# ScalarE decays retention's keys, the pairs' late products move to other PSUM banks, the solve follows retention's masks, and the chain loads a chunk ahead

## The chip, the cores and the metric

The kernel runs on one core of a Trainium2 chip. The metric is the device time of one execution in microseconds (us), the median of several runs.

## What is computed

One layer of a decoder: the input x (2048 tokens of 1024 numbers) is normalised, projected by one large matrix, and split among five branches (retention, GLA, a state-space branch, RWKV-7, attention into a memory); each branch's output is gated, projected up, weighted by a sigmoid gate, summed, projected out and added to x, and a last norm follows. The change touches retention and RWKV-7:

```
# retention, by chunks of 128 (one decay per head and step)
scores = einsum('bhntd,bhnsd->bhnts', qc, kc) * seg          # seg: the causal decay mask
y_intra = einsum('bhnts,bhnsv->bhntv', scores, vc)
chunk_state = einsum('bhnsd,bhnsv->bhndv', kc * exp(last - cum)[..., None], vc)   # decayed keys
y_inter = einsum('bhntd,bhndv->bhntv', qc * exp(cum)[..., None], prev)
# RWKV-7, one step per token
sa = einsum('bhvk,bhk->bhv', state, a_t)
state = state * w_t + sa[..., None] * b_t + v_t[..., None] * k_t
y_t = einsum('bhvk,bhk->bhv', state, r_t)
```

The kernel computes RWKV-7 by chunks of 64 tokens, so that the steps inside a chunk become a triangular system per head and chunk.

## The kernel before, in words

The 2048 tokens are worked in four groups of 512. Inside a group the order of the program is: memory attention; the preparation of RWKV-7's four pairs of heads (`rwkv_prep`); retention (`ret`, rotary of q, rotary of k, the value projection `v_tok`, then two pairs of heads, 0 and 1); the pairs' systems (`rwkv_sys`); RWKV-7's chain over eight chunks (`rwkv_chain`); the state-space branch; GLA; the output. Matmuls are full float32, made of three reduced ones over a high and a low part, so that a projection of one tile of 128 columns is 24 matmuls of 128x512 and a projection up from a branch is 6 on a half. Between the steps `fill(n)` takes n pieces of waiting work (gate projections with their tanh on ScalarE, and up projections, whose product VectorE merges into the tiles mg) off two lists, so that TensorE has something to do while other engines work.

- **Preparation.** For each pair, `rwkv_prep` projects k and r, then multiplies w2a2 into two PSUM banks of the pool br (L1108 to L1112), from which ScalarE and VectorE make the decays, the scaled a, b, k, r (tiles kb and ar, stored to DRAM as kbd and ard for the chain), and projects v. What is left for a pair, `late()` (L1158), runs inside the next pair's turn: 16 small matmuls into a bank (ap), which VectorE masks into ab (L299); a sum over heads into another bank (bps), which VectorE multiplies by v (L299); and four transposes of v into a third.
- **The solve.** When the last late is done, `rwkv_solve` sets up the triangular systems of 32x32 blocks, and 31 steps (n = 1 to 31) run on VectorE, each a product over n x n elements (L299 through `tt`) and a sum over it (L1206), both on tiles blk. `solve(n)` puts n steps into the program at the places where `ret` calls it: 4 (the setting up counts as one), 4, 6, then in each pair 4 and 6, and what is left at the start of `rwkv_sys`.
- **Retention's pairs.** For each pair `ret` makes qh on VectorE, transposes k into a br bank, multiplies by the decay kd into kt (L768, two VectorE instructions of 128x256 out of PSUM), makes the chunk states sp (TensorE, from kt), scores (TensorE), four states S and two masked scores (VectorE), y (TensorE), and in `finish_pair` two gate projections and, for each head, a sum of squares and a chain of ten VectorE instructions of 128x512 (L339, L329, L299, L302), whose result ScalarE casts (L378) and GpSimd splits.
- **The pairs' systems.** `rwkv_sys` transposes the solve's result twice (VectorE, L1222 and L1224), copies the parts (ScalarE and GpSimd, L1229), calls fill for 2 and 3 pieces, and joins the halves with 32x32 matmuls: lower, a VectorE copy zs (L1240), corner.
- **The chain.** In each chunk c, `rwkv_chain` issues loads of kbd, ard and vtd on the queue of the sync engine (SP), right before it uses them (L1271 to L1275).

What stands on each engine is not written by hand: a scheduler takes the program's instructions with their dependences and lays out one order per engine, and every engine works through its own in that order. PSUM has eight banks: a pool acc of three, br of three and y of two; a tile of a pool waits until the readers of the bank that it takes are done. SBUF's tiles s come from a pool of 42.

Names in the rows: L305 is the one line that issues all matmuls, L317 all transposes, L299 and L302 the VectorE products, L296 ScalarE's functions, L378 and L379 the split into high and low part (ScalarE, then GpSimd), L689 and L693 the GpSimd parts of the rotary, wt the weights' tiles (kw: their copy in DRAM, made in group 0 and loaded in groups 1 to 3).

## Time and profile before

| | |
|---|---|
| median of 3 runs | 3621.07 us (3617.41 to 3624.74) |
| the profiled execution's own time | 3618.59 us |
| its span | 3616.7 us |
| TensorE busy | 3428.6 us (95%) |
| VectorE, ScalarE, GpSimd busy | 55%, 28%, 25% |
| mean granted TensorE clock | 0.967 of full speed |

The profiled execution is 2.5 us below the median. To read the profile: idle time of TensorE is the span less its busy time, 188 us; a wait line tells which instruction of which engine ended such an idle stretch. PEclk is the TensorE clock that was granted, as a share of full speed; where it is below 1, busy time is longer than the same work takes at full speed.

### The profile page before, as it was taken

Reading aid. Unit: us, or ns where it says so; the run is one execution under the profiler, and the core shown is the slowest. Engines: PE = TensorE matmul, PEld = TensorE weight load, DVE = VectorE, ACT = ScalarE, POOL = GpSimd, SP = SyncE. Lnnn points to the kernel's source line nnn. Section 1 sums busy time; section 2 is a strip of 40 time slices with the busy share of each in tenths; the row PEclk is TensorE's granted clock in tenths of the full one; section 3 lists DMA queues with packets and bytes.
Section 4 is the critical chain, followed back from the end, with each engine's and each line's share of the span. In section 5 each row is a group of like instructions: output and inputs, shape, how many; then the busy total and the mean of one; then the engine's idle time right before and its main releaser. Section 6 shows DMA issues by size and latency. Waiting matters only on the chain.

```text
span 3616.7 us, 52010 instructions
## 1 busy us (share of the span) xinstructions
PE 3428.6 (95%) x20368; PEld 2760.3 (76%) x20368; DVE 1993.1 (55%) x3180; ACT 997.8 (28%) x1821; POOL 914.8 (25%) x919
## 2 busy tenths in 40 slices
PE   7879998998999899999999899999999989999998
PEld 6767777777777777888877787788887777778887
DVE  6785456635467645653357844554346674555243
ACT  5433224342343111312133121222123311131212
POOL 3665235555333110201103210021101411020110
PEclk9989899999999999999999999999999999999999
DMA  6665556576766454555565554445465654454555
GB/s 211 212 221 203 202 174 227 197 258 219 271 218 216 137 177 140 171 172 169 186 202 195 181 162 149 162 150 185 157 222 188 204 162 158 140 165 147 173 169 192
DMA packets 269541, 673.17 MB, mean 186 GB/s; under 512 B 27232, under 2 KB 81008, under 8 KB 269296
## 3 DMA queue, kind: packets, MB, share of 16 engines
q1 hardware_dynamic: 268864, 669.32, 55.6%
q8 instruction: 161, 2.64, 0.3%
q14 instruction: 84, 0.69, 0.1%
q10 hardware_dynamic: 432, 0.52, 0.1%
HBM read 503.54 MB, written 162.00 MB: 184 GB/s over the span
## 4 chain that ended last, share of the span: by engine, by line
PE 55%; DVE 10%; issue 1%; DMA 1%; ACT 1%; POOL 0%; SPq 0%; DVEq 0%; POOLq 0%; ACTq 0%
PE acc L305 44%; PE br L305 6%; PE y L305 4%; DVE s L302 4%; DVE s L299 2%; DVE blk L299 2%; DVE blk L1206 1%; PE br L317 1%; DMA s<-ard 1%; ACT s L296 1%; DVE s L339 0%; DVE s L329 0%; DMA s<-in_xT_dram 0%; ACT blk L1171 0%; DMA s<-kmd 0%
## 5 line engine op out<-in xcount | busy, mean ns | idle before, releaser
L305 PE MATMUL acc<-xhi,wt 128*128 128x512 f32 x5632 | 1820.9, 399 | 15.4 <-ACT s L296 9.6
L305 PEld LDWEIGHTS acc<-xhi,wt 128*128 128x128 f32 x5632 | 1071.5, 191 | 256.6 <-ACT s L296 12.3
L305 PE MATMUL acc<-xlo,wt 128*128 128x512 f32 x2816 | 1120.5, 398 | 2.5 <-DVE xlo L1552 1.8
L305 PEld LDWEIGHTS acc<-xlo,wt 128*128 128x128 f32 x2816 | 538.8, 191 | 117.2 <-DVE xlo L1552 3.0
L305 PE MATMUL acc<-s,wt 128*128 128x512 f32 (+1 forms) x2448 | 597.8, 394 | 15.1 <-DVE s L302 7.3
L305 PEld LDWEIGHTS acc<-s,wt 128*128 128x128 f32 x2448 | 456.3, 190 | 113.6 <-ACT wt L378 13.9
L302 DVE SCALAR_TENSOR_TENSOR s<-s,acc 128x512 f32<-128x512 f32 x192 | 131.6, 685 | 666.4 <-PE acc L305 360.7
L379 POOL TENSOR_TENSOR wt<-wr,wt 128x512 fp32r<-128x512 f32 (+1 forms) x256 | 354.8, 1391 | 380.1 <-ACT wt L378 369.3
L302 DVE SCALAR_TENSOR_TENSOR s<-s,s 128x512 f32<-128x512 f32 (+1 forms) x458 | 366.9, 805 | 31.9 <-ACT s L296 19.8
L379 POOL TENSOR_TENSOR s<-s,s 128x512 fp32r<-128x512 f32 x120 | 159.7, 1339 | 816.6 <-ACT s L378 672.3
L296 ACT ACTIVATE s<-acc 128x512 f32<-128x512 f32 x232 | 136.3, 595 | 593.4 <-PE acc L305 593.3
L305 PE MATMUL br<-s,s 64*64 64x64 f32 (+6 forms) x2432 | 213.1, 281 | 47.9 <-DVE s L768 26.9
L305 PEld LDWEIGHTS br<-s,s 64*64 64x64 f32 (+3 forms) x2432 | 164.3, 168 | 97.6 <-issue 39.8
L378 ACT CAST wt<-wr 128x512 fp32r<-128x512 f32 (+1 forms) x256 | 155.2, 611 | 268.3 <-PE acc L305 89.6
L1416 POOL TENSOR_TENSOR mg<-mg,s 128x512 f32<-128x512 f32 x64 | 87.2, 1362 | 548.6 <-DVE s L302 548.6
L378 ACT CAST s<-s 128x512 fp32r<-128x512 f32 x182 | 112.8, 620 | 341.4 <-DVE s L302 316.6
L296 ACT ACTIVATE s<-s 128x512 f32<-128x512 f32 (+1 forms) x204 | 119.3, 611 | 293.3 <-DVE s L299 114.1
L299 DVE TENSOR_TENSOR s<-s,s 128x512 f32<-128x512 f32 (+2 forms) x186 | 144.2, 803 | 44.5 <-ACT s L296 42.2
L299 DVE TENSOR_TENSOR s<-s 128x512 f32<-128x512 f32 (+1 forms) x167 | 163.0, 980 | 5.8
L305 PE MATMUL y<-s,s 128*64 128x64 f32 (+4 forms) x2112 | 137.2, 254 | 7.5 <-DVE s L299 4.9
L305 PE MATMUL acc<-wt,xhi 128*128 128x512 f32 x384 | 124.3, 404 | 19.0 <-DMA wt<-kw 9.0
L305 PEld LDWEIGHTS y<-s,s 128*64 128x64 f32 (+2 forms) x2112 | 113.4, 152 | 37.5 <-DVE s L1311 11.4
(220 smaller groups left out, 3202.5 us busy)
## 6 DMA issues: line engine op xcount, KB each, us to landing
wt<-kw SPq DMA_DIRECT2D x712, 512.0 KB, 3.3
kw<-wt SPq DMA_DIRECT2D x240, 512.0 KB, 3.0
wr<-in_wg_dram SPq DMA_DIRECT2D x176, 256.0 KB, 3.8
s<-in_xT_dram SPq DMA_DIRECT2D x88, 256.0 KB, 5.0
ard<-s SPq DMA_DIRECT2D x32, 256.0 KB, 2.2
kbd<-s SPq DMA_DIRECT2D x32, 256.0 KB, 2.7
s<-kbd SPq DMA_DIRECT2D x32, 256.0 KB, 4.1
s<-ard SPq DMA_DIRECT2D x32, 256.0 KB, 4.7
```

Of the source, the lines that this page charges most:

```text
L296: self.nc.scalar.activation(out, in_, f, bias=bias, scale=scale, **kw)
L299: self.nc.vector.tensor_tensor(out, a, b, op)
L302: self.nc.vector.scalar_tensor_tensor(out, a, s, b, op0, op1)
L305: i = self.nc.tensor.matmul(out, lhsT=lhsT, rhs=rhs, start=start, stop=stop)
L317: self.nc.tensor.transpose(out, in_, self.c["ident"])
L378: self.nc.scalar.copy(hi, src)
L379: (eng or self.nc.gpsimd).tensor_tensor(lo, src, hi.bitcast(F32), ALU.subtract)
L1206: nc.vector.tensor_reduce(X[:, s_, s_ + 1:], pv, AX.X, ALU.add)
L1416: (eng or self.pick({"ret": 0, "rwkv": 1, "ssd": 2, "gla": 3}[key])).tensor_tensor(merged[d], merged[d], t, ALU.add)
```

## The change

Four edits. The key decay of retention (L768) becomes two ScalarE activations with a scale instead of two VectorE multiplies. In `rwkv_prep` the w2a2 matmuls come before late, late's two banks that VectorE reads are taken from the pool y instead of br, and the first late has 2 pieces of fill ahead of it instead of 1. The first step of the `solve(4)` of a pair (step 14 in pair 0, step 24 in pair 1) carries a dependence on the pair's last mask, for the scheduler's order alone. The chain's three loads are issued one chunk ahead.

```diff
--- before.py
+++ after.py
@@ -280,7 +280,7 @@
 
     NS = 42
 
-    FILL = {"mem": (2, 0, 2, 2, 1, 1, 3, 3), "ret": (1, 3, 0), "late": (1, 1, 1, 1), "sys": (2, 3), "chain":
+    FILL = {"mem": (2, 0, 2, 2, 1, 1, 3, 3), "ret": (1, 3, 0), "late": (2, 1, 1, 1), "sys": (2, 3), "chain":
             (2, 3, 2, 1, 1, 2, 4, 3), "norm": 0, "ssd": (6, 0, 3, 4, 4), "gla": (3, 1, 2, 3, 1), "eng": (0, 1,
             0, 1, 0, 1, 0, 0, 1, 1, 1, 1, 1), "rope": (3, 3), "solve": (4, 4, 6, 4, 6)}
 
@@ -296,7 +296,7 @@
         self.nc.scalar.activation(out, in_, f, bias=bias, scale=scale, **kw)
 
     def tt(self, out, a, b, op):
-        self.nc.vector.tensor_tensor(out, a, b, op)
+        return self.nc.vector.tensor_tensor(out, a, b, op)
 
     def stt(self, out, a, s, b, op0, op1):
         self.nc.vector.scalar_tensor_tensor(out, a, s, b, op0, op1)
@@ -765,7 +765,7 @@
             for j in range(2):
                 h = 2 * p + j
                 v4 = lambda t: t.rearrange("p (c h d) -> p c h d", h=2, d=64)[:, :, j, :]
-                nc.vector.tensor_scalar(v4(kt), v4(tp), self.c["kd"][:, h:h + 1], None, ALU.mult)
+                self.act(v4(kt), v4(tp), AF.Copy, scale=self.c["kd"][:, h:h + 1])
 
             sp = self.ps("br")
             for c in range(4):
@@ -780,11 +780,11 @@
             for j, sps in enumerate(self.scores(k[p], q[p])):
                 pt = self.s()
                 h = 2 * p + j
-                self.tt(pt.rearrange("p (c t) -> p c t", t=P), sps.rearrange("p (c t) -> p c t", t=P),
+                i = self.tt(pt.rearrange("p (c t) -> p c t", t=P), sps.rearrange("p (c t) -> p c t", t=P),
                         self.c["dec"][:, h * P:(h + 1) * P].unsqueeze(1).to_broadcast([P, 4, P]), ALU.mult)
                 pts.append(pt)
             ys = [self.ps("y") for _ in range(2)]
-            self.solve(K.FILL["solve"][3])
+            self.solve(K.FILL["solve"][3], i)
             self.fill(K.FILL["ret"][0])
             for j in range(2):
                 for c in range(4):
@@ -1102,14 +1102,14 @@
             k = self.shift(4 + p)
             sq = self.squares(k, self.p["k_k"][:, pc], self.pick(6))
             r = self.shift(p)
-            if late:
-                self.fill(K.FILL["late"][i - 1])
-                late()
             wps, aps = self.ps("br"), self.ps("br")
             for t0 in range(0, T, 256):
                 t_ = slice(t0, t0 + 256)
                 self.mm(wps[:, t_], self.w2a2[0:64, cs_], wa[0:64, t_])
                 self.mm(aps[:, t_], self.w2a2[64:128, cs_], wa[64:128, t_])
+            if late:
+                self.fill(K.FILL["late"][i - 1])
+                late()
             pw = self.s()
             self.act(pw, wps, AF.Tanh, bias=self.hw0[:, pc], scale=0.5)
             nc.vector.tensor_scalar(pw, pw, 1.0, None, ALU.add)
@@ -1157,7 +1157,7 @@
 
             def late(i=i, p=p, rk=rk, v=v, ars=ars, kbs=kbs):
 
-                ap = self.ps("br")
+                ap = self.ps("y")
                 for c in range(8):
                     for q in range(2):
                         rq = slice(64 * q, 64 * q + 64)
@@ -1170,7 +1170,7 @@
                     rg, b = slice(32 * g, 32 * g + 32), g % 2
                     (nc.scalar.copy, nc.gpsimd.tensor_copy)[g % 2](
                         dia[rg, :, i * 8:i * 8 + 8], ab[rg, :, 32 * b:32 * b + 32].rearrange("s j t -> s t j"))
-                bps = self.ps("br")
+                bps = self.ps("y")
                 self.msum(bps, self.bones_r, rk)
                 bv = self.s()
                 self.tt(bv, bps, v, ALU.mult)
@@ -1198,19 +1198,22 @@
         nc.vector.memset(Xf[:, ::33], 1.0)
         prf = pr.rearrange("p s t -> p (s t)")
 
-        def step(s_):
+        def step(s_, after=None):
             n = 31 - s_
             pv = prf[:, 0:n * n].rearrange("p (c t) -> p c t", t=n)
-            self.tt(pv, X[:, s_ + 1:, s_ + 1:].rearrange("p t c -> p c t"),
+            i = self.tt(pv, X[:, s_ + 1:, s_ + 1:].rearrange("p t c -> p c t"),
                     blk[:, s_ + 1:, s_].unsqueeze(1).to_broadcast([P, n, n]), ALU.mult)
             nc.vector.tensor_reduce(X[:, s_, s_ + 1:], pv, AX.X, ALU.add)
-
-        return X, [lambda s_=s_: step(s_) for s_ in range(30, -1, -1)]
-
-    def solve(self, n=99):
+            if after is not None:
+                self.order(i, after)
+
+        return X, [lambda after=None, s_=s_: step(s_, after) for s_ in range(30, -1, -1)]
+
+    def solve(self, n=99, after=None):
         for _ in range(n):
             if self.dq:
-                self.dq.pop(0)()
+                self.dq.pop(0)(after)
+                after = None
 
     def rwkv_sys(self, Ab, X):
 
@@ -1266,13 +1269,20 @@
             b = self.s()
             nc.sync.dma_start(b, self.bvd[p])
             BV.append(b)
-        for c in range(8):
-            S = self.S_rw
+        def operands(c):
             AR, KB = self.s((P, 4, P)), self.s((P, 4, P))
             nc.sync.dma_start(KB, self.kbd[c])
             nc.sync.dma_start(AR, self.ard[c])
             UV = self.s((P, 8, 64))
             nc.sync.dma_start(UV[0:64], self.vtd[c * 64:c * 64 + 64, :, :].rearrange("t p (q d) -> t (p q) d", q=2))
+            return AR, KB, UV
+
+        nxt = operands(0)
+        for c in range(8):
+            S = self.S_rw
+            AR, KB, UV = nxt
+            if c < 7:
+                nxt = operands(c + 1)
             As = []
             aps = [self.ps("br") for _ in range(2)]
             for p, q, h, r in heads:
@@ -1364,7 +1374,7 @@
         Ab, dia, gC, late = self.rwkv_prep(wa, range(4))
         X = []
 
-        def begin():
+        def begin(_):
             late()
             x, self.dq = self.rwkv_solve(dia)
             X.append(x)
```

**TensorE, preparation of group 1, around the last pairs' w2a2.** Before, four products of late (64x64 and the sums over bones_r) stand ahead of w2a2 and all use br:

```order
L305 MATMUL br_2135_9860<-s_2110_9717,s_2111_9718 64x64 x8
L305 MATMUL br_2135_9860<-s_2112_9726,s_2113_9727 64x64 x8
L305 MATMUL br_2137_9883<-s_2103_9696,bones_r_441 128x512
L305 MATMUL br_2137_9883<-s_2104_9697,bones_r_441 128x512
L317 MATMUL br_2139_9889<-cst_76,s_2118_9768 128x128 x4
L305 MATMUL br_2141_9897<-s_1978_9088,w2a2_115 128x256 x2
L305 MATMUL br_2142_9898<-s_1978_9088,w2a2_115 128x256 x2
L305 MATMUL br_2152_9927<-s_2125_9809,bones_r_441 128x512
L305 MATMUL br_2152_9927<-s_2126_9810,bones_r_441 128x512
```

After, here one pair earlier, w2a2 comes first, a piece of fill (s is a branch's output, wt a weight) behind it, and then late in banks y:

```order
L305 MATMUL br_2088_9633<-s_1978_9088,w2a2_115 128x256
L305 MATMUL br_2089_9634<-s_1978_9088,w2a2_115 128x256
L305 MATMUL acc_2091_9641<-s_1940_8901,wt_2090_9639 128x512
L305 MATMUL acc_2091_9641<-s_1941_8902,wt_2090_9639 128x512
L305 MATMUL acc_2091_9641<-s_1940_8901,wt_2090_9639 128x512
L305 MATMUL acc_2091_9641<-s_1972_9049,wt_2090_9639 128x512
L305 MATMUL acc_2091_9641<-s_1973_9050,wt_2090_9639 128x512
L305 MATMUL acc_2091_9641<-s_1972_9049,wt_2090_9639 128x512
L305 MATMUL y_2093_9650<-s_2066_9501,s_2067_9502 64x64 x8
L305 MATMUL y_2093_9650<-s_2068_9510,s_2069_9511 64x64 x8
L305 MATMUL y_2095_9673<-s_2059_9480,bones_r_441 128x512
L305 MATMUL y_2095_9673<-s_2060_9481,bones_r_441 128x512
```

What moved: w2a2 no longer stands behind matmuls whose banks VectorE reads, and the fill stands between the two.

**VectorE, group 1, where retention's pair 0 begins.** Before, the solve's steps run to n = 30 ahead of qh (s<-s,cst) and the key decay (L768), and step 31 (128x961) right behind:

```order
L299 TENSOR_TENSOR blk_2194_10153<-blk_2193_10152,blk_2192_10150 128x900
L1206 TENSOR_REDUCE blk_2193_10152<-blk_2194_10153 128x30
L299 TENSOR_TENSOR s_2227_10390<-s_2166_9998,cst_76 128x512
L768 TENSOR_SCALAR s_2229_10397<-br_2228_10392,cst_76 128x4x64 x2
L302 SCALAR_TENSOR_TENSOR mg_2241_10448<-s_2087_9631,acc_2240_10441 128x512
L299 TENSOR_TENSOR blk_2194_10153<-blk_2193_10152,blk_2192_10150 128x961
L302 SCALAR_TENSOR_TENSOR s_2231_10409<-Sret_523_2368,cst_76,br_2230_10400 128x128
L1206 TENSOR_REDUCE blk_2193_10152<-blk_2194_10153 128x31
```

After, the steps stop after n = 13 (128x169): the four products of rotary k, qh, the four states (Sret) and the two masks follow, and step 14 (128x196) only behind these:

```order
L299 TENSOR_TENSOR blk_2197_10164<-blk_2196_10163,blk_2195_10161 128x169
L1206 TENSOR_REDUCE blk_2196_10163<-blk_2197_10164 128x13
L299 TENSOR_TENSOR s_2208_10237<-s_2200_10175,s_1922_8815 128x512
L299 TENSOR_TENSOR s_2209_10238<-s_2201_10176,s_1919_8804 128x512
L299 TENSOR_TENSOR s_2211_10247<-s_2201_10176,s_1922_8815 128x512
L299 TENSOR_TENSOR s_2212_10248<-s_2200_10175,s_1919_8804 128x512
L299 TENSOR_TENSOR s_2230_10401<-s_2170_10029,cst_76 128x512
L302 SCALAR_TENSOR_TENSOR s_2234_10420<-Sret_528_2384,cst_76,br_2233_10411 128x128
L302 SCALAR_TENSOR_TENSOR s_2234_10420<-s_2234_10420,cst_76,br_2233_10411 128x128 x2
L302 SCALAR_TENSOR_TENSOR Sret_2235_10421<-s_2234_10420,cst_76,br_2233_10411 128x128
L299 TENSOR_TENSOR s_2238_10436<-br_2236_10426,cst_76 128x512
L299 TENSOR_TENSOR s_2239_10438<-br_2237_10427,cst_76 128x512
```

What moved: steps 14 to 31 from ahead of pair 0 to behind it. Of these, steps 14 to 23 stand between pair 0's masks and its finish, and steps 24 to 31 behind pair 1's masks.

**VectorE, group 1, at the end of the solve.** After, the last step, the two transposes (L1225 and L1227 in the new numbering) and the start of pair 1's finish are interleaved; mg_2352 is the merge that frees the bank of acc_2351:

```order
L299 TENSOR_TENSOR blk_2197_10164<-blk_2196_10163,blk_2195_10161 128x961
L302 SCALAR_TENSOR_TENSOR s_2329_10909<-s_2328_10907,acc_2327_10882 128x512
L339 TENSOR_SCALAR s_2332_10915<-br_2330_10911 128x512
L1206 TENSOR_REDUCE blk_2196_10163<-blk_2197_10164 128x31
L329 TENSOR_SCALAR s_2331_10914<-s_2332_10915 128x512
L1225 STREAM_TRANSPOSE blk_2353_11005<-blk_2196_10163 128x1024
L299 TENSOR_TENSOR s_2333_10917<-s_2331_10914 128x512
L1227 STREAM_TRANSPOSE blk_2354_11007<-blk_2196_10163 128x1024
L302 SCALAR_TENSOR_TENSOR s_2333_10917<-s_2333_10917,s_2332_10915 128x512
L302 SCALAR_TENSOR_TENSOR s_2331_10914<-s_2333_10917,s_2331_10914 128x512
L302 SCALAR_TENSOR_TENSOR mg_2352_11003<-s_2310_10812,acc_2351_10996 128x512
L299 TENSOR_TENSOR s_2333_10917<-s_2331_10914 128x512
```

Before, the solve and its transposes were done ahead of pair 0's finish, and none of this stood beside pair 1's.

**ScalarE, group 1.** After, the new key decay of pair 1 (from br_2289, with the scale from cst) stands behind the two casts that end pair 0's finish:

```order
L378 CAST s_2278_10646<-s_2277_10644 128x512
L378 CAST s_2286_10668<-s_2285_10666 128x512
L296 ACTIVATE s_2290_10691<-br_2289_10686,cst_76 128x4x64 x2
```

and at the end of retention the copies of the solve's parts (L1232, L1229 before) and the two casts that end pair 1's finish stand ahead of the tanh of acc_2348:

```order
L296 ACTIVATE s_2328_10907<-acc_2327_10882 128x512
L1232 COPY s_2047_9440<-blk_2353_11005 32x8x32 x2
L1232 COPY s_2094_9667<-blk_2353_11005 32x8x32 x2
L1232 COPY s_2142_9914<-blk_2353_11005 32x8x32 x2
L1232 COPY s_2190_10141<-blk_2353_11005 32x8x32 x2
L378 CAST s_2336_10929<-s_2335_10927 128x512
L378 CAST s_2344_10951<-s_2343_10949 128x512
L296 ACTIVATE s_2349_10992<-acc_2348_10967 128x512
L296 ACTIVATE s_2361_11065<-acc_2360_11040 128x512
L296 ACTIVATE s_2365_11096<-acc_2364_11071 128x512
```

What moved: the decay from VectorE into ScalarE's order, and the eight copies from before retention's finish to here. TensorE's order behind retention's y of pair 1 is: projections acc_2322 and acc_2327 (24 each), four sums of squares, acc_2348 (24), acc_2351 and acc_2356 (6 each), acc_2360 and acc_2364 (24 each), then the systems' lower; acc_2360 waits for a VectorE reader of a bank and acc_2364 for a ScalarE reader.

## Rows read from the trace of the kernel before

**Rows 1.** The page, its first part: busy microseconds of an engine, its share of the span, its instructions.

```profile
PE 3428.6 (95%) x20368; PEld 2760.3 (76%) x20368; DVE 1993.1 (55%) x3180; ACT 997.8 (28%) x1821; POOL 914.8 (25%) x919
```

**Rows 2.** The waits of TensorE over the whole span: who was waited for, us in total, how often, the longest.

```profile
PE br L305 <- DVE s L768: 26.9, 5, 6.2
PE br L305 <- DVE s L299: 25.0, 12, 5.5
PE acc L305 <- DMA wt<-kw: 9.2, 6, 2.4
PE br L305 <- DMA s<-ard: 7.4, 10, 1.5
PE br L305 <- POOL s L1149: 6.3, 2, 3.1
```

**Rows 3.** Windows over the four preparations of the pairs (group 0 to 3): start and end, length, busy us and count of each engine, PEclk (the mean granted clock), share of the DMA engines, GB/s.

```profile
98.00:214.00 116.00, 105.01 (x545) 83.50 (x545) 90.45 (x112) 54.66 (x94) 85.10 (x95) 0.93 0.69 230
1052.00:1159.00 107.00, 102.82 (x541) 82.30 (x541) 80.92 (x119) 37.08 (x64) 46.45 (x67) 0.98 0.68 220
1909.00:2023.00 114.00, 106.39 (x561) 85.08 (x561) 83.55 (x123) 38.88 (x65) 46.72 (x68) 0.96 0.65 212
2779.00:2893.00 114.00, 106.25 (x553) 84.93 (x553) 83.58 (x123) 38.85 (x65) 46.73 (x68) 0.96 0.64 212
```

**Rows 4.** The waits of TensorE in three of these windows, the first, second and third group's, one line of each (the fourth has the same line as the third).

```profile
PE br L305 <- DVE s L299: 9.4, 3, 5.5
PE br L305 <- DVE s L299: 3.8, 2, 2.9
PE br L305 <- DVE s L299: 2.9, 1, 2.9
```

**Rows 5.** Windows in group 1, columns as in rows 3: around retention's first pair; as the pairs' systems begin.

```profile
1202.00:1213.00 11.00, 6.74 (x36) 5.40 (x37) 10.24 (x16) 0.00 (x0) 0.00 (x0) 0.53 0.04 17
1291.00:1298.00 7.00, 7.00 (x93) 5.44 (x88) 2.73 (x7) 1.85 (x6) 0.00 (x0) 0.52 0.55 189
```

**Rows 6.** The waits in the stretch of retention's value projection: two lines of TensorE's in group 0 (230 to 266 us), and one of GpSimd's in group 1 (1171 to 1198 us).

```profile
PE acc L305 <- POOL wt L379: 5.4, 3, 4.2
PE acc L305 <- ACT wt L378: 2.2, 1, 2.2
POOL s L689 <- DVE s L299: 13.3, 1, 13.3
```

**Rows 7.** The timeline of VectorE in group 1: start, us, engine, line, operation, out<-in. The solve's steps are the pairs of L299 and L1206 on blk; 128x196 is step 14, 128x576 step 24, 128x961 step 31.

```profile
1170.76 0.53 DVE L299 TENSOR_TENSOR blk<-blk,blk 128x196 f32<-128x196 f32 x1
1188.03 1.13 DVE L299 TENSOR_TENSOR blk<-blk,blk 128x576 f32<-128x576 f32 x1
1205.73 0.87 DVE L768 TENSOR_SCALAR s<-br,cst 128x256 f32<-128x256 f32 x2
1209.87 1.15 DVE L1206 TENSOR_REDUCE blk<-blk 128x31 f32<-128x961 f32 x1
1212.92 2.02 DVE L1222 STREAM_TRANSPOSE blk<-blk 128x1024 f32<-128x1024 f32 x1
1214.86 1.20 DVE L1224 STREAM_TRANSPOSE blk<-blk 128x1024 f32<-128x1024 f32 x1
```

**Rows 8.** The timeline of VectorE where retention is finished: the first row, a middle one and the last of the second head's chain of pair 1, in group 1 and then in group 0.

```profile
1280.29 0.68 DVE L339 TENSOR_SCALAR s<-br 128x512 f32<-128x512 f32 x1
1282.54 1.42 DVE L302 SCALAR_TENSOR_TENSOR s<-s,s 128x512 f32<-128x512 f32 x2
1286.95 0.69 DVE L302 SCALAR_TENSOR_TENSOR s<-s,s 128x512 f32<-128x512 f32 x1
356.05 0.68 DVE L339 TENSOR_SCALAR s<-br 128x512 f32<-128x512 f32 x1
359.57 3.36 DVE L302 SCALAR_TENSOR_TENSOR s<-s,s 128x512 f32<-128x512 f32 x2
366.97 0.69 DVE L302 SCALAR_TENSOR_TENSOR s<-s,s 128x512 f32<-128x512 f32 x1
```

**Rows 9.** ScalarE in group 1: a cast and a tanh from a PSUM bank (timeline), and a group of instructions of the whole span that reads 128x256 from PSUM (busy us, mean ns of one).

```profile
1255.27 0.62 ACT L378 CAST s<-s 128x512 fp32r<-128x512 f32 x1 [7.56 <-DVE s L302]
1270.62 0.60 ACT L296 ACTIVATE s<-acc 128x512 f32<-128x512 f32 x1 [3.41 <-PE acc L305]
L1294 ACT COPY rs<-br 128x256 f32<-128x256 f32 x32 | 11.9, 372 | 48.0 <-PE br L305 48.0
```

**Rows 10.** The timeline of TensorE in group 1, retention's pair 1: two matmuls of a projection with two others between them; states and scores; the first half of y.

```profile
1251.86 0.39 PE L305 MATMUL acc<-xlo,wt 128*128 128x512 f32 x1
1252.54 0.39 PE L305 MATMUL acc<-xlo,wt 128*128 128x512 f32 x1
1256.94 2.95 PE L305 MATMUL br<-s,s 128*64 128x128 f32 x32
1261.08 2.05 PE L305 MATMUL y<-s,s 128*128 128x128 f32 x16
```

**Rows 11.** Windows, columns as in rows 3: retention of group 0 and of group 1, and the start of the pairs' systems of group 0.

```profile
266.00:366.00 100.00, 88.03 (x516) 71.33 (x514) 60.49 (x72) 32.15 (x58) 54.18 (x45) 0.91 0.60 204
1198.00:1286.00 88.00, 81.76 (x424) 66.84 (x422) 52.75 (x76) 16.77 (x28) 14.12 (x15) 0.94 0.45 141
366.00:382.00 16.00, 13.31 (x183) 10.53 (x184) 7.34 (x16) 5.12 (x12) 2.56 (x2) 0.57 0.61 192
```

## The prediction

> **What bounds the kernel now.** I read the page first: TensorE is busy 95% of the span, 3428.6 of 3616.7 us [rows 1], so time can be won only from its 188 us of idle time and from the stretches in which a stall is followed by a lowered clock. Then its waits: the largest are for the key decay (26.9 us in 5 waits), for VectorE's masks while TensorE wants a br bank (25.0 in 12), for weights from DRAM (9.2), the chain's loads (7.4) and GpSimd's part of late's operands (6.3) [rows 2]. The change aims at each of them. Then windows, for the clock: around the wait for the key decay in group 1 the mean granted clock is 0.53, and TensorE is busy 6.74 us of 11 [rows 5]; at about half speed (1.2 instead of 2.4 GHz), 0.47 x 6.74 = 3.2 us of that busy time would not be there at full speed. So a stall of 6 us costs about 9. I price each clock loss so: (1 - PEclk) x busy.
>
> **A. Preparation.** w2a2 waits for a br bank because late's two products hold two of three until VectorE has read them, and VectorE is behind. The four windows hold 11.0, 4.2, 7.6 and 7.8 us of idle time (length less PE busy), 30.5 in all, and 7.4 + 2.1 + 4.3 + 4.3 = 18.1 us of clock loss [rows 3]. After, w2a2 stands ahead of late, and late uses y. The upper bound is thus 48.6 us; the lower is the named waits alone, 9.4 + 3.8 + 2.9 + 2.9 [rows 4] + 6.3 (POOL s L1149, covered by the added piece of fill) [rows 2] = 25.3. The named stalls sit inside most of the lowered stretches, so I take 38. A piece of fill taken here is missing later, but it is work that has to be done anyway; cost nil.
>
> **B. Value projection.** In group 1, GpSimd's rotary part waits 13.3 us for VectorE [rows 6], whose four products stand among solve steps; the rotary's stores stand in SP's queue ahead of the weights, so TensorE then waits for wt. After, step 13 is the last ahead of these products, and steps 14 to 23, from 1170.76 to 1188.03 [rows 7], are out of their way. TensorE's waits: most of the 9.2 us for wt<-kw [rows 2] and 5.4 + 2.2 in group 0 [rows 6], 16.8; with a clock loss in group 0 that I don't see apart it could be 22, and if the loads themselves are late, 0. I take 17. The chain's prefetch adds no load here: its loads come later in SP's order.
>
> **C. Retention's pairs.** For pair 0 the decay ran at 1205.73, behind step 30 [rows 7]. After, it is on ScalarE, ahead of the whole queue of steps. A read of 128x256 from PSUM takes ScalarE 372 ns [rows 9], VectorE 0.43 (0.87 for two [rows 7]): the engine itself changes nothing, only the queue does. Of the 26.9 us [rows 2], four waits (22.7) are pair 0's; four clock losses of 3.2 go with them: -35.5, and about 0.8 per group comes back for transposes, decay and states in a row, +3: -32.
>
> For pair 1, the decay on ScalarE stands behind two casts that need the end of pair 0's finish. That finish, on VectorE, is two chains of some 7.4 us (1280.29 to 1287.64 for such a one [rows 8]) with a merge between, 15.7, then cast 0.62 [rows 9] and two decays, 0.74: 17.1 us after the sums of squares. TensorE's work from there to the states is now two projections and two 6-matmul pieces, 60 matmuls at 0.68/3 = 0.227 us each [rows 10], 13.6. So TensorE waits about 2.6 (17.1 less 13.6 and less 0.9 for transposes and the late start), then about 1.2 for the masks (states and scores take 2.95, y starts 4.1 after them with four matmuls between [rows 10]), and loses about 1.7 of clock: +5.5 in groups 1 to 3. In group 0 a wait and clock loss of 7.5 is there already; I get 12: +4.5. Together +21.
>
> **D. The pairs' systems, the new cost.** Let t1 be the end of pair 1's masks. VectorE then has steps 24 to 31 (1188.03 to 1211.02 less 2.7 for what stood between [rows 7]: 20.3), two merges and two finish starts (2.4), the transposes with two rows between (2.02 + 1.20 + 1.1 [rows 7]), two products (1.4), then mg_2352 (0.6): t1 + 29. TensorE does y (2.05 for one half [rows 10], 1.0 for the smaller one, an estimate), two projections of 24 matmuls (5.45 each at 0.227), four sums of squares, one projection and two pieces: 3.1 + 10.9 + 0.9 + 5.45 + 2.7 = 23.0, and acc_2360 then waits for mg_2352: 6.4 to 7. VectorE's rest of two chains ends 11 us later, t1 + 40; cast 0.62 and tanh 0.60 [rows 9], so acc_2364's bank is free at t1 + 41.3, while acc_2360 was done at t1 + 34.9: 6.4 more. Clock loss behind the second stall 3.2; zs and corner 0.6. Against it stands the lowered clock of before, 0.48 x 7.0 = 3.4 [rows 5]. Net 7 + 6.4 + 3.2 + 0.6 - 3.4 = +13.8 in groups 1 to 3. In group 0 the chains are slower, 11.6 us against 7.35 for the second [rows 8]; with 7 us more for both and the steps, and 8.4 of stall and clock there before (2.7 idle and 0.43 x 13.31 [rows 11]), I take +14.5. Together +56.
>
> Here lies the rule that speaks against the change. The row order shows the decay and the tanh behind casts that wait for VectorE, though their own operands are ready; the trace shows such a cast only after an idle stretch of 7.56 us that VectorE ended [rows 9].
>
> The Trainium skill, PSUM — Partial Sum Buffer, Engine vs sequencer instructions, says that ScalarE's and VectorE's queues are strictly first in, first out. By that rule the tanh waits out both chains, as in my sum. Were a ready instruction let past, the sum would lose 6.4 + 3.2 in four groups, some 38 us.
>
> **E. Chain.** Loads a chunk ahead remove most of 7.4 us [rows 2]; bounds 0 and 10 with clock; I take 6. The loads move ahead of 2 or 3 weight loads of fill in SP's queue; 512 KB land in about 3 us each by the page, and the pieces have a projection's time in hand: nil.
>
> **Sum.** -38 - 17 - 32 + 21 + 56 - 6 = -16 against the profiled 3618.6: 3602.6; the median is 2.5 above that execution, so **3605**. A measurement tells 0.2%, 7.2 us, from no change.
>
> **Rivals.**
>
> *Slower: retention's chains run at group 0's pace in every group.* In group 0 two products of two SBUF tiles take 3.36 us where GpSimd splits weights beside them, in group 1 1.42 [rows 8]. After, the eight GpSimd copies of the solve's parts fall beside pair 1's chains, and each chain now sits on TensorE's path. If all of group 0's slowdown came, 4.3 us for the second chain [rows 8], 2 for the first, 2 for the steps and 4 where the decay waits, it were +12.3 in three groups: 3605 + 37 = **3642**. It decides from 8 us per group. Against it: GpSimd is busy 14 of 88 us in retention of group 1, 54 of 100 in group 0 [rows 11].
>
> The Trainium skill, GPSIMD Engine Reference, Specifications, has the cause of such a slowdown: GpSimd shares its SBUF interfaces with VectorE, with contention where a VectorE instruction has two SBUF inputs. The rows agree; by the rule only the 5.5 us of copies could slow a chain here, +3 per group, or 3614.
>
> *Same: the early gains come short.* If B gives nothing, since wt is late by itself, or A gives its lower bound, 25, the sum loses 13 to 17, **3618 to 3622**. Against it: the waits name VectorE's reads as releasers, and these leave the path.
>
> *Much faster: the work behind the masks covers the solve.* If VectorE's order leaves the merges and the tanh no later than TensorE needs them, the second stall of D goes: 3605 - 4 x (6.4 + 3.2) = **3567**. Against it: the casts stand ahead of the tanh in the row order.
>
> *The change does not do what it says*, the wait for the decay being taken over by one just as long: +32, **3637**. Against it: ScalarE has only the copies of V ahead of pair 0's decay.
>
> **How the numbers follow.** Forecast (3590 to 3614) 0.48; much faster 0.12; same 0.20; slower by the chains 0.13; not as it says 0.07. From 3614 to 3628 is within 0.2%. Faster 0.57 (some of the same case lies just above it), same 0.22, slower 0.21. The range reaches into both outer cases and leaves out about half of each: 3567 to 3637. The likeliest one's own is 3590 to 3614.
>
> **What would show it.** Right: no wait for L768's successor in pair 0; no br wait for L299 in the four preparations and a clock near 1 there; wt<-kw and s<-ard nearly gone from the waits; one wait of about 3 us for ScalarE ahead of pair 1's states; two waits of 6 to 7 us per group ahead of the pairs' systems, one for VectorE's merge (mg) and one for ScalarE's tanh, with a clock near half behind. Wrong: no stall after pair 1's masks (then much faster), or chains of over 10 us per head in groups 1 to 3 (then slower).

## The result and the profile after

The changed kernel takes 3665.23 us (median of 4, 3657.98 to 3671.73) against 3619.24 us for the kernel before (4 runs): a ratio of 1.0129, interval 1.0109 to 1.0148. It is 46 us slower by the medians (47 by the ratio), where 14 us faster was forecast, and it lies above the range (3567 to 3637). The profiled execution took 3657.98 us.

The page after, its span and TensorE's line, against [rows 1]:

```profile
span 3656.2 us, 52064 instructions
...
PE 3454.0 (94%) x20368; PEld 2766.5 (76%) x20368; DVE 1998.9 (55%) x3164; ACT 1005.0 (27%) x1837; POOL 928.7 (25%) x919
```

The span is 39.5 us longer with the same 20368 matmuls. TensorE is busy 25.4 us longer, which can only be clock and pace (the mean granted clock is 0.963 instead of 0.967), and idle 202.2 us instead of 188.1. TensorE's waits over the span, against [rows 2]:

```profile
PE acc L305 <- ACT s L296: 35.9, 10, 9.5
PE acc L305 <- DVE mg L302: 19.9, 4, 6.1
PE br L305 <- ACT s L1182: 19.8, 12, 4.1
PE br L305 <- ACT s L296: 19.1, 6, 8.3
PE acc L305 <- DMA wt<-kw: 17.8, 9, 3.2
...
PE br L305 <- DVE s L299: 7.3, 3, 4.9
...
PE y L305 <- POOL s L1149: 5.3, 2, 3.4
```

Most of what was meant to go went: there is no wait for L768's successor in pair 0, 7.3 us instead of 25.0 for VectorE while a br bank is wanted, and no wait for s<-ard. GpSimd's part of late's operands stayed: 5.3 of 6.3 us, now in front of a y bank. And other waits stand in the place of those that went: tanh (35.9 us; that line was 9.6 before), merges (mg, 19.9), the copy L1182 of late's transposed v (19.8), the decay (ACT s L296 to br, 19.1, most of it ahead of pair 1's states: 8.3 in group 0 and 2.7 in each of the others), and weights, 17.8 instead of 9.2. To see where the time is lost I cut both spans 2 us ahead of the first w2a2 of each group. The four windows, before and then after (columns as in rows 3):

```profile
0.00:1052.00 1052.00, 948.14 (x5395) 753.25 (x5396) 620.25 (x900) 392.18 (x735) 503.70 (x434) 0.94 0.64 216
1052.00:1909.00 857.00, 834.92 (x5034) 673.13 (x5033) 470.56 (x778) 209.52 (x381) 137.32 (x162) 0.99 0.54 177
1909.00:2779.00 870.00, 844.11 (x5034) 680.54 (x5033) 473.31 (x782) 210.93 (x382) 137.17 (x163) 0.97 0.53 174
2779.00:3616.70 837.70, 801.45 (x4911) 653.37 (x4909) 428.94 (x725) 185.15 (x324) 136.63 (x161) 0.97 0.52 170
```

```profile
0.00:1052.00 1052.00, 945.12 (x5394) 748.98 (x5395) 626.44 (x896) 392.77 (x739) 508.17 (x434) 0.94 0.64 216
1052.00:1932.00 880.00, 848.49 (x5035) 679.53 (x5035) 471.25 (x774) 211.80 (x385) 140.30 (x162) 0.98 0.53 172
1932.00:2809.00 877.00, 850.47 (x5034) 681.16 (x5033) 472.89 (x777) 213.15 (x386) 140.89 (x163) 0.97 0.52 173
2809.00:3656.20 847.20, 809.90 (x4909) 656.85 (x4907) 428.30 (x720) 187.29 (x328) 139.36 (x161) 0.97 0.51 168
```

Group 0 is as long as before, groups 1 to 3 are 23, 7 and 9.5 us longer.

At the preparation, the timeline after in group 1 (VectorE, ScalarE, TensorE) shows what replaced the wait for VectorE:

```profile
1116.02 0.68 DVE L299 TENSOR_TENSOR s<-y,cst 128x512 f32<-128x512 f32 x1
...
1116.73 1.26 ACT L1171 COPY blk<-s 32x256 f32<-32x256 f32 x2 [2.56 <-DVE s L299]
...
1118.02 0.59 ACT L1182 COPY s<-br 128x512 f32<-128x512 f32 x1
...
1118.65 0.73 PE L305 MATMUL br<-s,bones_r 128*128 128x512 f32 x2 [3.36 <-ACT s L1182]
```

w2a2 now holds two br banks and late's transposes the third, so the sum over squares (br<-s,bones_r) waits 3.36 us until ScalarE has copied v (L1182), and that copy stands behind ScalarE's copies L1171, which wait for VectorE's mask. Ahead of the systems in group 1 (1262 to 1302 us) stand the two waits that the prediction put at 7 and 6.4 us:

```profile
PE acc L305 <- DVE mg L302: 6.1, 1, 6.1
PE acc L305 <- ACT s L296: 5.0, 1, 5.0
```

### The profile page after: what moved, and what is told of

Read it like the earlier page. It is cut to its first block, busy times and chain, and to the rows that moved or that the text cites. A ratio compares the mean times of both kernels' runs of the same rounds, so it can differ in the third digit from the quotient of the medians.

```text
span 3656.2 us, 52064 instructions
## 1 busy us (share of the span) xinstructions
PE 3454.0 (94%) x20368; PEld 2766.5 (76%) x20368; DVE 1998.9 (55%) x3164; ACT 1005.0 (27%) x1837; POOL 928.7 (25%) x919
## 5 line engine op out<-in xcount | busy, mean ns | idle before, releaser
L305 PE MATMUL acc<-xhi,wt 128*128 128x512 f32 x5632 | 1841.2, 401 | 74.5 <-ACT s L296 35.9
L305 PE MATMUL acc<-s,wt 128*128 128x512 f32 (+1 forms) x2448 | 611.7, 399 | 15.5 <-DVE s L302 7.5
L302 DVE SCALAR_TENSOR_TENSOR s<-s,acc 128x512 f32<-128x512 f32 x192 | 131.6, 685 | 609.8 <-PE acc L305 352.0
L379 POOL TENSOR_TENSOR wt<-wr,wt 128x512 fp32r<-128x512 f32 (+1 forms) x256 | 354.8, 1391 | 368.0 <-ACT wt L378 350.6
L302 DVE SCALAR_TENSOR_TENSOR s<-s,s 128x512 f32<-128x512 f32 (+1 forms) x458 | 373.4, 819 | 31.8 <-ACT s L296 19.6
L379 POOL TENSOR_TENSOR s<-s,s 128x512 fp32r<-128x512 f32 x120 | 166.3, 1394 | 849.8 <-ACT s L378 762.4
L296 ACT ACTIVATE s<-acc 128x512 f32<-128x512 f32 x232 | 136.5, 596 | 719.6 <-PE acc L305 702.7
L378 ACT CAST wt<-wr 128x512 fp32r<-128x512 f32 (+1 forms) x256 | 155.3, 611 | 283.1 <-PE acc L305 107.8
L305 PE MATMUL br<-s,s 64*128 64x128 f32 (+5 forms) x1920 | 192.9, 291 | 22.0 <-ACT s L296 16.5
L305 PEld LDWEIGHTS br<-s,s 64*128 64x128 f32 (+3 forms) x1920 | 145.8, 171 | 72.7 <-issue 35.4
L296 ACT ACTIVATE s<-s 128x512 f32<-128x512 f32 (+1 forms) x204 | 119.3, 610 | 295.5 <-DVE s L299 115.9
L378 ACT CAST s<-s 128x512 fp32r<-128x512 f32 x182 | 112.7, 620 | 310.1 <-DVE s L302 270.7
L299 DVE TENSOR_TENSOR s<-s,s 128x512 f32<-128x512 f32 (+2 forms) x186 | 152.3, 846 | 50.0 <-ACT s L296 40.7
L305 PE MATMUL y<-s,s 128*64 128x64 f32 (+5 forms) x2624 | 162.6, 252 | 15.9 <-DVE s L299 8.1
L305 PEld LDWEIGHTS y<-s,s 128*64 128x64 f32 (+3 forms) x2624 | 135.7, 152 | 50.7 <-DVE s L299 12.4
L299 DVE TENSOR_TENSOR s<-s 128x512 f32<-128x512 f32 (+1 forms) x167 | 154.4, 928 | 5.2
```

The lines of the kernel that those rows point to most:

```text
L296: self.nc.scalar.activation(out, in_, f, bias=bias, scale=scale, **kw)
L299: return self.nc.vector.tensor_tensor(out, a, b, op)
L302: self.nc.vector.scalar_tensor_tensor(out, a, s, b, op0, op1)
L305: i = self.nc.tensor.matmul(out, lhsT=lhsT, rhs=rhs, start=start, stop=stop)
L378: self.nc.scalar.copy(hi, src)
L379: (eng or self.nc.gpsimd).tensor_tensor(lo, src, hi.bitcast(F32), ALU.subtract)
```

## The experiments

Each ran 5 rounds beside the kernel before; times are medians, ratios are to the kernel before with their 95% interval.

**The four edits one by one.** e1 has the edit of the solve alone, e2 the decay alone, e3 the preparation's three edits, e4 the chain's loads:

```diff
 e1: self.solve(K.FILL["solve"][3], i)    # and step(after), as in the diff
 e2: self.act(v4(kt), v4(tp), AF.Copy, scale=self.c["kd"][:, h:h + 1])
 e3: w2a2 ahead of late; ap and bps = self.ps("y"); "late": (2, 1, 1, 1)
 e4: nxt = operands(c + 1)
```

> The kernel before with the solve's order alone (later half behind retention's masks); the decay stays on VectorE, the preparation and the chain's loads as before. Theory 1 (the solve's tail behind pair 1's masks, and the ScalarE and PSUM queue behind it, is the main loss; the stages from retention to the systems lost some 50 us in the trace after): pair 0's waits for the decay go, but two waits of 4 to 6 us per group stand ahead of the systems: slower by 35 to 50 us. Rival 2 (the decay on ScalarE, behind the casts, makes the stalls): without it the stalls go and pair 0's gain stays, 20 to 35 us faster than before.

> The kernel before with the key decay on ScalarE alone. Theory 1: the wait for the decay goes, but states and masks of pair 0 still stand behind steps 30 and 31 on VectorE, so TensorE waits for the masks instead: within 8 us of before. Rival 2: the decay behind pair 0's casts makes TensorE wait about 3 us in each group's pair 1: slower by 10 to 20 us.

> The kernel before with the preparation's edit alone (w2a2 ahead of late, late's two products in y, one more piece of fill). Theory 1: VectorE's waits are traded for waits of the same kind, the sum over squares now waiting for the br bank of late's transposes, which ScalarE copies only behind copies that wait for VectorE's mask; and weights wait where rotary k begins: within 10 us of before. Rival 3 (the preparation's edit is the main loss): slower by 15 us or more. What I had predicted for it: 38 us faster.

> The kernel before with the chain's loads a chunk ahead alone. Theory 1: the stage sums of the two traces (idle time and clock loss in the four chains) fell by about 23 us: faster by 12 to 23 us. Rival 4 (that fall is a matter of where lowered clock stretches happened to lie): faster by no more than the 7 us of named waits.

| | median us | ratio |
|---|---|---|
| e1, solve's order | 3625.01 | 1.0020 (1.0008 to 1.0033) |
| e2, decay on ScalarE | 3613.39 | 0.9989 (0.9977 to 1.0001) |
| e3, preparation | 3668.07 | 1.0139 (1.0117 to 1.0162) |
| e4, chain's loads | 3594.58 | 0.9940 (0.9921 to 0.9959) |

The theory with which I came from the two traces (theory 1), that the solve's tail is the main loss, falls: alone it costs 7 us. Rival 2, which had e1 faster by 20 to 35 us and e2 slower by 10 to 20, falls too. Rival 3 holds: the preparation's edit alone is as slow as the whole change. e2 is as theory 1 had it: TensorE waits for VectorE's masks (y) in the place of the decay, in the waits of e2:

```profile
PE y L305 <- DVE s L299: 34.7, 17, 7.2
```

e1 does bring the wait for the merges ahead of the systems, in its waits over the span:

```profile
PE acc L305 <- DVE mg L302: 42.0, 8, 8.1
```

but it takes the four waits of pair 0 away, so little is left. e4 is faster by 22 us, at the upper end of theory 1's interval. The chain of group 1 in the kernel before and in e4 (columns as in rows 3):

```profile
1299.00:1418.00 119.00, 113.67 (x1221) 88.85 (x1220) 59.04 (x110) 20.50 (x41) 11.26 (x8) 1.00 0.43 142
```

```profile
1288.00:1403.00 115.00, 114.09 (x1216) 87.94 (x1215) 55.37 (x109) 20.73 (x41) 10.62 (x8) 1.00 0.43 141
```

Cut at the same places, the 119 us of this group's chain became 115, with 0.9 us idle instead of 5.3. In groups 2 and 3, 121 and 120 us became 115 each, and group 0's chain, from the first matmul on its state (Srw) to the last, takes 112.0 us instead of 118.5: some 21 us in the four chains, nearly all that e4 gains. Only 1.7 of the 5.3 us were named waits for the loads (s<-ard); 3.1 were waits of the transposes for VectorE (L317 <- DVE s L299), of which 0.4 are left in e4.

**The preparation's three edits one by one**, and the change without them:

```diff
 e5: -"late": (1, 1, 1, 1)   +"late": (2, 1, 1, 1)
 e6: the four w2a2 lines ahead of "if late:", late in br
 e7: -ap = self.ps("br"), bps = self.ps("br")   +ap = self.ps("y"), bps = self.ps("y")
 e8: the changed kernel with rwkv_prep and "late" as before
```

> The kernel before with one number changed: two pieces of fill instead of one ahead of the first late. Theory F (the added piece shifts every later piece by one, so that weights, tanh and merges fall due where nothing covers them; the weights' waits rose from 9.2 to 25.3 us and the tanh's from 9.6 to 26.1 in the run with the preparation's edit alone): slower by 20 to 45 us. Theory W (w2a2 ahead of late takes two br banks, late's transposes the third, so the sum over squares waits for ScalarE's copy): within 10 us of before.

> The kernel before with w2a2 ahead of late alone; late's products stay in br, one piece of fill. Theory W: the sum over squares (and late's own products) still wait for a br bank, now for ScalarE's tanh and copy: slower by 15 to 45 us. Theory F: within 10 us of before, since the fill is as it was. What I had predicted from w2a2's place: faster.

> The kernel before with late's two products in the pool y alone; w2a2 stays behind late. w2a2 then finds two br banks that VectorE does not hold: faster by 10 to 25 us by the 25 us of waits for VectorE's masks and products, if those waits are for banks. By theory W, which puts the harm in w2a2's place, the same. If the pool y itself is the trouble (the value projection and retention's y take its banks), no gain or slower.

> The changed kernel without the preparation's edit: decay on ScalarE, the solve's order, the chain's loads. If the edits add up (+7, -4, -24 us alone): faster than before by 15 to 25 us. If the decay on ScalarE and the solve's order make the stalls only together (decay behind the casts, tanh behind the casts, as in the changed kernel, where the stages from retention to the systems lost 50 us): within 10 us of before or slower.

| | median us | ratio |
|---|---|---|
| e5, one more piece | 3657.67 | 1.0118 (1.0100 to 1.0137) |
| e6, w2a2 first | 3626.90 | 1.0034 (1.0020 to 1.0049) |
| e7, banks in y | 3600.58 | 0.9957 (0.9943 to 0.9972) |
| e8, no preparation | 3598.72 | 0.9950 (0.9935 to 0.9966) |

One number, 1 to 2, makes 43 us. The two parts of the preparation that I had priced are smaller, and of opposite sign: w2a2's place costs 12 us, the banks give 16. 12 is neither theory W's 15 to 45 nor theory F's "within 10". In e7 the wait for VectorE is 6.5 us, where [rows 2] has 25.0, and part of it comes back as a wait for ScalarE's copy:

```profile
PE br L305 <- ACT s L1182: 10.9, 12, 4.2
...
PE br L305 <- DVE s L299: 6.5, 5, 4.7
```

The rest of it comes back in smaller waits: over its span e7 is idle for 186.3 us (3595.5 less 3409.2 busy), against 188.1 before. What fell is busy time, by 19.4 us, at a mean granted clock of 0.972 instead of 0.967. So in these two executions the banks' gain is hardly one of idle time; it shows as less time at the lower clock ((1 - PEclk) x busy: 113.1 us before, 95.5 in e7).

e8 is 18 us faster: the solve, the decay and the chain add up (7 - 4 - 22 = -19). So the second case of its expectation, that these make the stalls together, falls, and the loss comes with the preparation.

In e6, w2a2 no longer waited for VectorE, but late's own products did, and their operands weren't ready either:

```profile
PE br L305 <- DVE s L299: 26.7, 20, 4.8
...
PE br L305 <- POOL s L1149: 14.5, 5, 6.3
```

Why does the piece of fill cost so much? The waits of e5 are up at places far behind the first late:

```profile
PE br L305 <- DVE s L768: 46.8, 8, 8.3
PE acc L305 <- ACT s L296: 26.0, 10, 6.2
...
PE acc L305 <- DMA wt<-kw: 19.7, 12, 4.9
```

Before, these lines were 26.9, 9.6 and 9.2: 47 us more in three lines. The list of waiting pieces is made by `inter`, which alternates a gate projection (24 matmuls) and a projection up (6 matmuls), with two gate projections at its start and two projections up at its end; a call `fill(1)` takes the next one. With one more taken in the first late, nearly every later call gets the other kind, until the list is emptied behind the group's chain. Here is TensorE in group 1 between retention's sums of squares of pair 0 and the states of pair 1, before (the rows left out are matmuls of gate projections):

```profile
1237.99 1.07 PE L305 MATMUL br<-s,ones_r 128*128 128x512 f32 x4
1238.91 0.60 PE L317 MATMUL br<-cst,s 128*128 128x128 f32 x4
1239.26 1.64 PE L305 MATMUL acc<-s,wt 128*128 128x512 f32 x6
...
1246.19 1.52 PE L305 MATMUL acc<-s,wt 128*128 128x512 f32 x6
...
1256.94 2.95 PE L305 MATMUL br<-s,s 128*64 128x128 f32 x32
```

After the transposes (L317) came 6 matmuls, 24, 6, and 41 of the next 48 (a piece of 24, and the start of the pair's own gate projections): 18.0 us, from 1238.91 to 1256.94, until the states. The same place in e5:

```profile
1255.75 1.07 PE L305 MATMUL br<-s,ones_r 128*128 128x512 f32 x4
1256.66 0.60 PE L317 MATMUL br<-cst,s 128*128 128x128 f32 x4
...
1262.59 1.52 PE L305 MATMUL acc<-s,wt 128*128 128x512 f32 x6
...
1269.39 1.52 PE L305 MATMUL acc<-s,wt 128*128 128x512 f32 x6
1273.56 4.66 PE L305 MATMUL br<-s,s 128*64 128x128 f32 x31 [2.65 <-DVE s L768]
```

Now it is 24, 6, 24, 6: 60 matmuls instead of 77, 13.6 us of them, and a wait of 2.65 us for the decay, here still on VectorE. And in the changed kernel:

```profile
1235.89 1.08 PE L305 MATMUL br<-s,ones_r 128*128 128x512 f32 x4
1236.80 0.60 PE L317 MATMUL br<-cst,s 128*128 128x128 f32 x4
...
1242.69 1.52 PE L305 MATMUL acc<-s,wt 128*128 128x512 f32 x6
...
1249.49 1.52 PE L305 MATMUL acc<-s,wt 128*128 128x512 f32 x6
1253.73 2.95 PE L305 MATMUL br<-s,s 128*64 128x128 f32 x32 [2.72 <-ACT s L296]
1257.79 2.05 PE L305 MATMUL y<-s,s 128*128 128x128 f32 x16 [1.10 <-DVE s L299]
```

the same pieces and nearly the same wait (2.72), now for ScalarE, and 1.10 for the masks.

**Is it the swap, or the piece itself?** Two runs on the kernel before give the piece back, or take one more; e11 and e13 do so in the changed kernel:

```diff
 e9:  "late": (2, 0, 1, 1)   in the kernel before
 e10: "late": (3, 1, 1, 1)   in the kernel before
 e11: "late": (1, 1, 1, 1)   in the changed kernel
 e13: "late": (3, 1, 1, 1)   in the changed kernel
```

> The kernel before with 2, 0, 1, 1 pieces of fill ahead of the four lates (before: 1, 1, 1, 1): the added piece is given back at the second late. Theory P (waiting pieces alternate, 24 matmuls and 6 matmuls; one more taken swaps long and short ones at every later place, so retention's pairs and the systems get short cover where they had long): from the second late on all is as before, so within 12 us of before. Theory I (the piece hurts where it stands, in the first late): as slow as with 2, 1, 1, 1, by 30 to 45 us.

> The kernel before with 3, 1, 1, 1 pieces: two more than before in the first late. Theory P: long and short pieces stand again where they stood, each place only has the next pair's: within 15 us of before. Theory S (each piece taken early is missing where the lists run dry later): slower than with 2, 1, 1, 1, by 45 us or more over before.

> The changed kernel with the one number taken back (1, 1, 1, 1). Theory P: the swap of long and short pieces is what turned the change around; without it the other edits give what they gave apart (+7, -4, -24, -16 us, and w2a2's place between -10 and +12): faster than before by 20 to 45 us. Rival W (w2a2 ahead of late and the solve's tail make the loss between them): within 10 us of before or slower.

> The changed kernel with 3, 1, 1, 1 pieces instead of 2, 1, 1, 1. Theory P (long and short pieces swap places at every later call when one more is taken, and stand right again when two more are): though still more is taken early, it comes back to near the changed kernel with 1, 1, 1, 1: faster than before by 5 to 30 us. If in the changed kernel it is another matter (pieces missing later, or the first late itself): as slow as the changed kernel or slower, 40 us or more over before.

| | median us | ratio |
|---|---|---|
| e9, 2, 0, 1, 1 | 3621.19 | 1.0016 (1.0004 to 1.0028) |
| e10, 3, 1, 1, 1 | 3620.48 | 1.0009 (1.0001 to 1.0018) |
| e11, changed, 1, 1, 1, 1 | 3601.53 | 0.9959 (0.9946 to 0.9971) |
| e13, changed, 3, 1, 1, 1 | 3610.58 | 0.9985 (0.9972 to 0.9997) |

One more piece costs 43 us, two more 3, and one more given back at the next call 6. So neither the work missing later nor the place is the cause: it is which kind of piece stands where. TensorE's order in the traces agrees, in all four groups: between pair 0's sums of squares and pair 1's states stand 6, 24, 6 and then gate projections in the kernel before, e9, e10, e11 and e13, and 24, 6, 24, 6 in e3, e5, e14 and the changed kernel. Ahead of the systems two more pieces are not the same as none, since one list ends there with two projections up and the next begins with two gate projections: in e13 TensorE waits 13.0 us there in group 1: 4.6 us for VectorE and 8.4 us for retention's own output to be split (L378, L379), which the next list's projections up need. In the changed kernel the number alone is worth 61 us (1.0129 against 0.9959), and e13 brings back most of it. With 1, 1, 1, 1 the changed kernel is 15 us faster than before, less than the 20 to 45 expected. It is also what I had forecast for the whole, but by luck: w2a2's place and the banks, which were to give 38 us, give nothing beside the other edits (e11 0.9959, e8 without them 0.9950), and the other three edits, which were to cost 22 together (-17 - 32 + 21 + 56 - 6), gain 18 (e8).

Ahead of the systems of group 1, e11 waits for merges only (1255 to 1276 us):

```profile
PE acc L305 <- DVE mg L302: 9.1, 2, 6.6
```

The tail of the solve does cost there, 9.1 us as against 11.1 in the changed kernel, but the wait for the tanh, and the 2.72 us ahead of pair 1's states, are not there: they came with the swap.

**Does the swap cost more beside the solve's tail?**

```diff
 e14: kernel before + solve's order + decay on ScalarE + "late": (2, 1, 1, 1)
```

> The kernel before with the solve's order, the decay on ScalarE and 2, 1, 1, 1 pieces; preparation's order, banks and the chain's loads as before. The parts alone were +7, -4 and +43 us. If they add: slower by 40 to 50 us. Theory X (the solve's tail and the casts on ScalarE are covered only while the long pieces stand behind them, so the swap costs more with them): slower by 55 to 75 us.

3656.36 us, ratio 1.0110 (1.0091 to 1.0128): 40 us. The parts add, nearly (7 - 4 + 43 = 46), and theory X falls. What stays open: the parts alone, the preparation's edit counted as three, sum to 7 - 4 - 22 + 43 + 12 - 16 = +20 us, and the changed kernel is at +47. The preparation's three sum to 39 and measure 50 together (e3). The rest, some 15 us, I can't assign. As e8 and e14 add, it lies in what the preparation's edits do beside the others; the larger waits for weights (25.3 us in e3, 17.8 in the changed kernel) are a candidate that no run here isolates.

**A version from it.** It has the chain's loads ahead, the decay on ScalarE, late's products in y, w2a2 and the fill as before, and another cut of the solve:

```diff
-"solve": (4, 4, 6, 4, 6)
+"solve": (4, 4, 16, 4, 4)
-self.solve(K.FILL["solve"][3], i)
+self.solve(K.FILL["solve"][3], i if p == 0 else None)
```

> A version from the findings: before, with the chain's loads ahead, the decay on ScalarE, late's products in y, the fill as before, w2a2 behind late as before, and the solve cut elsewhere: 16 instead of 6 steps put behind the value projection (so that steps 1 to 23 run ahead of pair 0) and only step 24 tied to pair 0's masks, nothing to pair 1's. Steps 24 to 31 and the transposes, some 25 us, then fall between pair 0's masks and its finish, where VectorE sat idle for about 17 us of some 27. -24 (chain), -16 (y), -20 to -35 (pair 0's waits for the decay and their clock), little back: faster than before by 45 to 75 us. If VectorE's finish of pair 0 is late by it, and pair 1 waits: by 25 to 40.

3573.34 us, ratio 0.9876 (0.9859 to 0.9893): 45 us faster than before, at the low end of the expectation. In its waits the merges are down to 2.9 us; of the waits for the decay one of 6.6 us in group 0 and one of 1.6 in group 3 are left. The largest line is a cost of the new cut, 20.9 us where it was 7.7 before: between pair 0's sums of squares and pair 1's states TensorE waits for a bank that VectorE reads (L302), 3.9 us in group 0 and 3.0 in each other group. In group 1 that product (1219.37) waits for a tanh of ScalarE, which runs right behind the copies of the solve's parts (L1232, 5.27 us from 1213.38):

```profile
PE acc L305 <- DVE s L302: 20.9, 9, 6.5
PE br L305 <- ACT s L1182: 14.5, 12, 4.2
...
PE br L305 <- ACT s L296: 10.7, 5, 6.6
...
PE br L305 <- DVE s L299: 8.9, 6, 3.7
...
PE acc L305 <- DVE mg L1426: 2.9, 1, 2.9
```

In group 1, steps 18 to 23 run beside TensorE's value projection (1159.8 to 1182.8; steps 1 to 17 just ahead of it), and steps 24 to 31 and the transposes from 1188.5 to 1214.5, between pair 0's masks and its finish (from 1220.6), so the systems (from 1267.4) find it done.

## Why the prediction was wrong

- **The failed step is the last sentence of A**: "A piece of fill taken here is missing later, but it is work that has to be done anyway; cost nil." I priced the number by its work. Its price is in the order behind it: 43 us alone (e5), 61 in the changed kernel (e11). These 61 us are as much as the whole distance from the forecast (-14) to the result (+47); the other misses, listed below, cancel. I had the evidence under my eyes: in C I counted 60 matmuls "now" ahead of pair 1's states, and took it as a fact of the new order instead of asking how many stood there before (77) and what had made the difference.
- **A's gain was mis-sized too.** I took 38 us; the banks give 16 (e7), and w2a2's place loses 12 (e6). I named what would release w2a2, but did not follow who takes the third br bank next: the transposes, freed by ScalarE's copy, which waits for VectorE. ScalarE's order, on which D rests, I did not follow here. At the place itself nothing was gained. From a group's first w2a2 to its value projection TensorE is idle (length less PE busy) for 32.8 us in the four groups before, 43.0 after, and 40.2 in e11, which has the preparation's other two edits without the piece. The sums over the four stretches, in this order:

```profile
sum 494.10, PE 461.31 PEld 370.34 DVE 369.83 ACT 177.08 POOL 236.38; mean PE 115.33 PEld 92.58 DVE 92.46 ACT 44.27 POOL 59.10
sum 511.50, PE 468.47 PEld 369.84 DVE 373.23 ACT 178.97 POOL 235.51; mean PE 117.12 PEld 92.46 DVE 93.31 ACT 44.74 POOL 58.88
sum 498.30, PE 458.08 PEld 361.90 DVE 374.59 ACT 178.50 POOL 236.93; mean PE 114.52 PEld 90.48 DVE 93.65 ACT 44.62 POOL 59.23
```

- **B held at its place.** From first to last matmul the value projections took 37.0, 26.1, 26.2 and 25.5 us before, and 31.3, 22.3, 22.1 and 21.9 with the solve's order alone (e1): 17 us, as forecast. In the changed kernel they are 17 us shorter too, but weights are waited for elsewhere.
- **C and D were right in the changed kernel, but half of it for a cause that I did not see.** Pair 0's waits went; 2.6 and 1.2 us ahead of pair 1 were 2.72 and 1.10; 7 and 6.4 ahead of the systems were 6.1 and 5.0 (the working of D gives 29 less 23.0, 6.0, and the sum took 7 for it). The tanh ran at 1300.56, right behind the second chain's cast (1300.03), as D had it. But I put all of these to the solve's tail and ScalarE's order. The wait for merges is the solve's tail, and is there with the fill as before (9.1 us in e11); the waits ahead of pair 1's states in groups 1 to 3 and the wait for the tanh came with the swap. Without the swap C and D cost less than forecast: from the end of the value projection to the chain's first step the four groups took 454.7 us in e8 and 432.1 before, 23 us more where 45 were forecast (-32 + 21 + 56).
- **E was too small**: 22 us instead of 6 (e4). I took the named waits for loads; these were only a part of what the late loads held up: 4 to 6.5 us went in the chain of each group, some 21 in all.
- **The rivals.** The slower one that I gave (chains at group 0's pace) is not it: its time, 3642, is 23 us below the measured one, and its mechanism was absent. The second head's chain of pair 1 took 8.0 us in group 1 (1292.03 to 1300.00), near the 7.35 before and not group 0's 11.6. The one that happened, an edit that changes nothing but a number and reorders all that follows, I did not list.

## What to carry to other kernels

When work waits in a list and the program takes it by count, a changed count is not an edit at one place: it shifts which piece covers which wait at the later calls, and with pieces of two sizes in turn an odd shift swaps long cover for short. Price it by walking the later calls, or keep the count neutral by giving the piece back at the next one. And when a change is a bundle, look in the new order for differences that no edit in the bundle explains; each of them has a cause that has not been priced yet.

## What the runs showed of the hardware that was not expected

How much of a stall's price is clock. The same 20368 matmuls kept TensorE busy 3405.4 us in e12 and 3454.0 us in the changed kernel, at mean granted clocks of 0.976 and 0.963: of the 84 us between their spans (3572.1 and 3656.2), 49 are longer busy time and only 35 idle time. Priced as (1 - PEclk) x busy, 127.8 us less 81.7, the time at the lower of the two granted levels (1.2 instead of 2.4 GHz) accounts for 46 of the 49. Counting the waits alone would have shown less than half of the difference. In e7 it would have shown next to nothing: 1.8 us of idle time and 19.4 of busy time went.
